# A two-layer decoder trunk in which stored weight remainders change queue and an out-projection's gates, next norm and first mixes change place

## The chip, the cores and the metric

The kernel runs on one core of a Trainium2 chip. The time is the device time of one execution in microseconds (us); the number to predict is the median of several executions. The program works with five engines, each with an instruction queue of its own that is worked through in order: TensorE (PE in the profile, its weight loads PEld), VectorE (DVE), ScalarE (ACT), GpSimd (POOL) and SyncE (SP, which only issues DMAs).

## What is computed

The input has 512 tokens of width 1024; 16 learned meta tokens are put ahead, which makes 528 rows. There are two layers, each with a half-weighted SwiGLU block, a mixer and another such block, with an RMS norm ahead of each. The mixer of layer 0 is RWKV-7 time mixing, that of layer 1 sparse attention. The change lies in layer 0:

```python
xx = shift(h) - h
xr, xw, xk, xv, xa, xg = h + xx * mix          # six mixes of the normed rows
r, k, v = xr @ w_r, xk @ w_k, xv @ w_v
w_log = -softplus(-(w0 + tanh(xw @ w1) @ w2)) - 0.5
a = sigmoid(a0 + (xa @ a1) @ a2)
g = sigmoid(xg @ g1) @ g2                      # the gate
y = wkv7_scan(...)
out = ((norm(y) + bonus) * g) @ w_o            # gate, then out-projection
```

All is float32 in and out.

## The kernel before

**Numbers as pairs.** A float32 product is made of three matmuls in a faster 32-bit format (`mm3`, line 597): each operand x is split into a rounded part hi (ScalarE copies x into the format) and the remainder lo (VectorE subtracts hi from x), and w_hi x_hi, w_hi x_lo and w_lo x_hi are added in one PSUM bank. The tokens are worked in two ranges, A (272 rows) and B (256 rows), channels down the partitions, so a matmul has a 128x128 weight block and 272 or 256 columns.

**Weights** (class `Weights`, from line 201). All weights lie in DRAM as units of 128x1024, in the order in which TensorE takes them, eight blocks to a unit. A unit is loaded by SP into one of four buffers `wraw`, ScalarE writes `whi`, VectorE writes `wlo` (four buffers each); `take` (line 271) splits two units ahead of use, three where a store is near. Some units are used again later in the program. For these, `wlo` is computed once and stored in DRAM (tiles `lo...`), and later loaded instead of being computed (`back`, line 256; groups `lo<-wlo` and `wlo<-lo` of the profile). There are 32 such stores: 12 of units that the first block uses itself (kind "keep"), 14 of projection units that are split early, between the first block's own units, and only stored there (kind "save", every fourth place of the order from unit 27), and 6 of out-projection units ("keep"). A `wlo` buffer that is stored is free for its next unit only when the store has landed. The store is issued in `split` (line 253) right behind the subtraction. 26 of the stores lie in the first 210 us, the other 6 in the first out-projection.

**Order.** The text of the program is the order of every engine. A planner (`run`, line 862, with the model `Clock`) puts the steps of side chains between the matmuls of a main stream. `early` (line 890) puts the statistics of the next norm into a stream: at step `at` the column sums (`Norm.stat`: matmuls with `ones` into a `bg` bank, then a Newton iteration of some 12 small VectorE instructions on a tile `nst`), and some steps later (`apart`) the spread to 128 partitions (matmuls with `ident`, copied by ScalarE into `rstd`).

**The out-projection** (`outproj`, line 1488) is called for range A in `joined` (line 1579), after the second half of a SwiGLU block for range B, and later for range B. `gate(m)` makes five matmuls into one of three `bg` banks, VectorE multiplies the bank with the scan's result (tile `AR`) into a tile `tb`, and `split` writes hi (ScalarE, rows `p<-tb` of ACT) and lo (VectorE, rows `p<-tb,p` of DVE). Gates 0, 1 and 2 come first; then for d = 0 to 7 gate d+3 and the nine matmuls of block d into three `acc` banks (columns m = 0, 1, 2); then columns 3 to 7, each with 24 matmuls into one `acc` bank. There are four `acc` banks, used in turn. At the end of a column VectorE adds the bank to the residual stream (rows `h<-acc,h`, called h0 to h7 here), ScalarE squares it and VectorE adds the square to `ss`.

**The next projection** (`proj`, line 948) starts inside that stream: `joined` takes a step of it at three places of the out-projection. Each of these steps makes one mix (`mix`, line 964): VectorE norms a channel block (`ynat<-h,vecs,rstd`), subtracts (`bu<-ynat`) and mixes (`tb<-bu,vecs,ynat`); hi and lo follow in the next two mixes. When the out-projection is done, the projection takes its four accumulators from the four `acc` banks, which columns 4, 5, 6 and 7 of the out-projection used last, and for each channel block d it does 12 matmuls, three for each accumulator.

Of the kernel before, what the change touches and what calls it, by code (L numbers as in the profile page):

```python
# [10 lines left out]
F32 = mybir.dt.float32  # L11
F32R = mybir.dt.float32r
I32 = mybir.dt.int32
AF = mybir.ActivationFunctionType
# [11 lines left out]
B = (272, 528)  # L26
# [25 lines left out]
def blk(key, k, m):  # L52
    return (key, k, m * 128, (m + 1) * 128)
# [149 lines left out]
class Weights:  # L203
# [35 lines left out]
    def split(self, last):  # L239

        while self.nlo <= min(last, len(self.units) - 1):
            u = self.nlo
            self.round(u)
            self.back(u)
            r = self.raw.pop(u)
            w = r.shape[1]
            if self.kind[u] != "again":
                lo = self.pool.tile([128, 1024], F32R, name="wlo", bufs=self.bufs)
                self.nc.vector.tensor_sub(lo[:, :w], r, self.hi[u][:, :w].bitcast(F32))
                self.lo[u] = lo  # L250
            if self.kind[u] in ("save", "keep"):
                d = self.saved[self.key[u]] = self.dram.tile([128, 1024], F32, name=f"lo{self.key[u]}")
                self.nc.sync.dma_start(d, lo.bitcast(F32))
            self.nlo += 1

    def back(self, last):
# [278 lines left out]
def trunk(ctx, tc, wall, plan, h0, vec, cstd, gqk, out, stop=None, gap=0.0, share=400.0, slack=200.0, fulls={}):  # L535
    clock = Clock()
    nc = Core(tc.nc, clock)
    @contextmanager
    def tile_pool(name, bufs=1, **kw):
        with tc.tile_pool(name=name, bufs=bufs, **(kw if "space" in kw else dict(reuse_waits="tile", **kw))) as pool:  # L540
            yield Pool(pool, bufs, clock)
# [46 lines left out]
    def col(c):  # L588
        return vecs[:, c:c + 1]

    def bank():
        return psum.tile([128, 512], F32, name="acc", bufs=4)

    def bbank(tag="bg"):
        return psum.tile([128, 512], F32, name=tag, bufs={"bg": 3, "ry": 1}[tag])

    def mm3(p, w, x, first, last):

        nc.tensor.matmul(p, w[0], x[0], start=first, stop=False)
        nc.tensor.matmul(p, w[0], x[1], start=False, stop=False)  # L600
        nc.tensor.matmul(p, w[1], x[0], start=False, stop=last)

    def split(hi, lo, src):
        nc.scalar.activation(hi, src, AF.Copy)
        nc.vector.tensor_sub(lo, src, hi.bitcast(F32))
# [103 lines left out]
    def residual(m, r, p, c):  # L709
        s = slice(*r)  # L710
        nc.vector.scalar_tensor_tensor(h[:, m, s], p, c, h[:, m, s], op0=OP.mult, op1=OP.add)
# [178 lines left out]
    def early(main, norm, r, at=12, X=None, start=0, every=4, apart=0):  # L890


        steps = spread = None
        due = 10 ** 6
        own = Chain(None)

        def mine(f, *a):
            clock.chain = own
            x = f(*a)
            clock.chain = None  # L900
            return x

        for i, c in enumerate(main):
            if i == at:
                spread = mine(norm.stat, r)
            elif i > at + apart and spread and own.ready + gap < clock.t["tensor"]:
                spread = mine(spread)
                due = i + 3
            if X and i >= start and i > at and not spread and (own.ready - 800 <= clock.t["tensor"] or i >= due):
                steps = steps or norm.steps(X(), r)  # L910
                mine(next, steps, None)
                due = i + every
            yield c
        if spread:
            spread()
        if X:
            steps = steps or norm.steps(X(), r)
            for _ in steps:
                pass


    class Range:
# [14 lines left out]
        def spread(self, dst, p, f, **kw):  # L937

            nc.scalar.activation(dst[:, :8], chunks(p[:, :256]), f, **kw)
            if self.pad:  # L940
                nc.scalar.activation(dst[:, 8, :self.pad], p[:, 256:], f, **kw)
# [3 lines left out]
    def chunks(ap):  # L945
        return ap.rearrange("p (c t) -> p c t", t=CH)

    def proj(R, norm, pairs, core, ahead, park=None):

        r, pad, nch = R.r, R.pad, R.nch  # L950
        n = R.n - pad
# [10 lines left out]
        xm, slot, late = {}, {}, []  # L962
# [29 lines left out]
        def mixes(k):  # L992
            while k and queue and pairs.free:
                i, d = queue.pop(0)
                if i == 2:
                    norm.apply(d, r, hn[d][:, 1:1 + n])
                    nc.vector.tensor_sub(xx[d // 4][:, d % 4, :n], hn[d][:, 0:n], hn[d][:, 1:1 + n])
                mix(i, d)
                if (i, d) == (5, 3) and park:
                    park.move(nc, core.tile([128, 2, 2, 256], F32R, name="bu", bufs=2))  # L1000
                if not queue:
                    R.have.add("mixed")
                if i == 2 and pad and d % 4 == 3:
                    nc.scalar.activation(hnlast[:, d - 3:d + 1], hn2[d // 4][:, :, n:n + 1], AF.Copy)
                k -= 1
# [19 lines left out]
        if pad:  # L1025
            for t in (R.BKV[:, :, 8, 1:3, pad:], R.P[:, :, 8, 1 + pad:], R.a[:, :, n:288]):
                nc.gpsimd.memset(t, 0.0)
        for _ in range(4 if park else 3):
            mixes(1)
            yield  # L1030

# [43 lines left out]
        for kind, *st in proj_steps():  # L1075
# [19 lines left out]
            elif kind == "lora":  # L1095
                key, d = st
# [15 lines left out]
            else:  # L1112
                d = st[0]
# [374 lines left out]
    def outproj(R, pairs, nxt, last=None):  # L1488

        r = R.r  # L1490
        n = R.n - R.pad
        shi, slo = (t for _, t in R.gates)
        xs, slot = {}, {}

        def gate(m):
            p = bbank()
            mm3(p[:, :n], W.take(blk("g2", 0, m)), (shi[:, 0, :n], slo[:, 0, :n]), True, False)
            w = W.take(blk("g2", 1, m))
            nc.tensor.matmul(p[:, :n], w[0], shi[:, 1, :n], start=False, stop=False)
            nc.tensor.matmul(p[:, :n], w[1], slo[:, 1, :n], start=False, stop=True)  # L1500
            t = work.tile([128, 288], F32, name="tb", bufs=4)
            y = R.AR[:, m, :, 1]
            nc.vector.scalar_tensor_tensor(chunks(t[:, :256]), y[:, :8], col(LNB + m), chunks(p[:, :256]),
                                           op0=OP.add, op1=OP.mult)
            if R.pad:
                nc.vector.scalar_tensor_tensor(t[:, 256:n], y[:, 8, :R.pad], col(LNB + m), p[:, 256:n],
                                               op0=OP.add, op1=OP.mult)
            slot[m] = pairs.take()
            xs[m] = [slot[m][1][:, j, :n] for j in range(2)]
            split(*xs[m], t[:, :n])  # L1510

        def end(m, p):
            residual(m, r, p[:, :n], 1.0)
            nxt.add(m, r)

        for m in range(3):
            gate(m)
            yield
        ps = [bank() for _ in range(3)]
        for d in range(DT):  # L1520
            if d + 3 < DT:
                gate(d + 3)
            if d + 3 == DT - 1:
                for t in R.gates:
                    pairs.give(t)
                if last:
                    last()
            for m in range(3):
                mm3(ps[m][:, :n], W.take(blk("wo", d, m)), xs[d], d == 0, d == DT - 1)
            yield  # L1530
        for m in range(3):
            end(m, ps[m])
        for m in range(3, DT):
            p = bank()
            for d in range(DT):
                mm3(p[:, :n], W.take(blk("wo", d, m)), xs[d], d == 0, d == DT - 1)
                if m == DT - 1:
                    pairs.give(slot[d])
                yield
            end(m, p)  # L1540


    norms = [Norm(i, "ry" if i == 2 else "bg") for i in range(6)]
# [35 lines left out]
    def joined():  # L1579

        main = proj(RB, norms[1], pairs, core, stepsA)
        for i, c in enumerate(early(outproj(RA, pairs, norms[2]), norms[1], B, at=9, apart=4)):
            if i in (27, 31, 35):
                assert B in norms[1].rstd
                next(main)
            yield c
        yield from early(main, norms[2], A, at=100, apart=16)

    mid, right = ExitStack(), ExitStack()
    pairs = Pairs(right.enter_context(tile_pool("pairs", side="right")), 14)  # L1590
# [5 lines left out]
    RA, RB = Range(A), Range(B)  # L1596
# [8 lines left out]
    def prefix(main):  # L1605
# [10 lines left out]
        for i, c in enumerate(main):  # L1616
# [7 lines left out]
            yield c  # L1624

    run(prefix(proj(RA, norms[1], pairs, core, stepsB, HB)), "pA")
    ffn_stage(0, 0, B, norms[1], "f00b", XB, stepsB, xdone=gates(RA), HID=HB, part="rest")
    drain()
# [12 lines left out]
    def first_x(main):  # L1641
# [8 lines left out]
        for _ in steps:  # L1650
            pass

    run(early(first_x(outproj(RB, pairs, norms[2], after)), norms[3], A, at=9, apart=4))
    right.close()
    xq = xa[0]

    hid = ctx.enter_context(tile_pool("hid"))
    at = ctx.enter_context(tile_pool("at"))
# [456 lines left out]
```

## Time and profile before

| | us |
|---|---|
| median of 3 runs | 2252.68 (2248.6 to 2252.9) |
| profiled execution | 2253.37 |
| its span | 2251.6 |
| TensorE busy | 2209.3 |
| VectorE busy | 1643.9 |
| ScalarE busy | 1261.6 |
| GpSimd busy | 70.5 |

The profile is one execution. A row of a timeline has the start in us, the length, engine, line, operation, tiles written and read, and how often it stands there in a row; in brackets the idle time of the engine before it, and what ended it. Every instruction of this program has line 387, a wrapper, so tiles tell them apart. Matmuls overlap, so from one start to the next is the time that one takes (0.126 us for 272 columns). DMA issues are on the queue of SP or POOL; "to landing" is from issue until the data is there.

### The profile page before, as it was taken

How to read it: one execution, taken by the hardware profiler on the slowest of the kernel's cores; microseconds unless marked ns; L12 is line 12 of the kernel's file. 1: busy time of each engine (PE TensorE's matmuls, PEld its weight loads, DVE VectorE, ACT ScalarE, POOL GpSimd, SP SyncE). 2: the span in 40 equal slices, each digit the busy share in tenths (PEclk: the TensorE clock that was granted, in tenths of full speed). 3: DMA queues.
4: the chain of work that ended last, by engine and by line, in shares of the span. 5: the costliest groups of instructions: out<-in, count | busy, mean ns of one | idle time of the engine just before them, and what ended most of it. 6: DMA issues, size and time to landing. Idle time of an engine off the chain costs nothing.

```text
span 2251.6 us, 49304 instructions
## 1 busy us (share of the span) xinstructions
PE 2209.3 (98%) x20028; PEld 2147.2 (95%) x20028; DVE 1643.9 (73%) x3281; ACT 1261.6 (56%) x2189; POOL 70.5 (3%) x122
## 2 busy tenths in 40 slices
PE   8999999999999999999999999999999999999999
PEld 8999999999899999999999999899998989989999
DVE  7777787846878883676656659887667988867665
ACT  6555784486478447654445445556545645555443
POOL 0000002011000110000000000000000000000000
PEclk9999999999999999999999999999999999999999
DMA  8788766622585562365555655553455543435654
GB/s 283 276 295 280 277 217 236 197 68 88 198 296 177 161 195 79 103 221 185 178 172 167 194 164 169 164 172 129 144 180 162 172 151 106 149 104 179 191 184 140
DMA packets 115188, 405.66 MB, mean 180 GB/s; under 512 B 12993, under 2 KB 17169, under 8 KB 114961
## 3 DMA queue, kind: packets, MB, share of 16 engines
q1 hardware_dynamic: 112592, 397.07, 53.0%
q0 software_dynamic: 2368, 5.44, 0.9%
q8 instruction: 157, 2.57, 0.5%
q14 instruction: 71, 0.57, 0.1%
HBM read 380.88 MB, written 21.05 MB: 179 GB/s over the span
## 4 chain that ended last, share of the span: by engine, by line
PE 82%; DVE 10%; ACT 4%; issue 2%; DMA 1%; SPq 0%; ACTq 0%; DVEq 0%
PE acc L387 70%; PE bg L387 9%; PE ry L387 4%; DVE wlo L387 3%; DMA wraw<-wall 1%; ACT whi L387 1%; DVE tb L387 1%; DVE ynat L387 1%; DVE p L387 1%; DVE rel L387 1%; DVE h L387 1%; DVE m L387 0%; ACT pr L387 0%; DVE AR L387 0%; ACT p L387 0%
## 5 line engine op out<-in xcount | busy, mean ns | idle before, releaser
L387 ACT ACTIVATE whi<-wraw 128x1024 fp32r<-128x1024 f32 (+2 forms) x674 | 705.6, 1052 | 412.0 <-PE acc L387 244.3
L387 DVE TENSOR_TENSOR wlo<-wraw,whi 128x1024 fp32r<-128x1024 f32 (+3 forms) x628 | 766.1, 1223 | 187.8 <-ACT whi L387 173.4
L387 PE MATMUL acc<-p,whi 128*128 128x272 f32 (+1 forms) x4112 | 790.0, 291 | 14.6 <-ACT whi L387 6.7
L387 PEld LDWEIGHTS acc<-p,whi 128*128 128x128 f32 x4112 | 644.9, 190 | 23.7 <-DVE p L387 7.2
L387 PE MATMUL acc<-p,wlo 128*128 128x272 f32 (+1 forms) x2056 | 590.4, 287 | 0.2 <-DVE wlo L387 0.2
L387 PEld LDWEIGHTS acc<-p,wlo 128*128 128x128 f32 x2056 | 389.8, 190 | 0.6 <-DVE wlo L387 0.6
L387 PE MATMUL acc<-xa_hi,whi 128*128 128x256 f32 (+1 forms) x1072 | 306.6, 286 | 0.0
L387 PE MATMUL acc<-xa_hi,wlo 128*128 128x256 f32 (+1 forms) x1072 | 304.3, 284 | 1.0 <-DVE wlo L387 1.0
L387 PE MATMUL acc<-xa_lo,whi 128*128 128x256 f32 (+1 forms) x1072 | 303.7, 283 | 0.0
L387 PE MATMUL acc<-hid_hi,whi 128*128 128x256 f32 (+1 forms) x880 | 253.0, 288 | 1.3 <-DVE ta L387 1.0
L387 PE MATMUL acc<-hid_lo,whi 128*128 128x256 f32 (+1 forms) x880 | 250.1, 284 | 4.3 <-DVE hid_lo L387 4.3
L387 PE MATMUL acc<-hid_hi,wlo 128*128 128x256 f32 (+1 forms) x880 | 249.9, 284 | 0.0
L387 PE MATMUL acc<-xb_hi,whi 128*128 128x256 f32 x744 | 211.3, 284 | 0.0
L387 PE MATMUL acc<-xb_hi,wlo 128*128 128x256 f32 x744 | 208.7, 280 | 0.0
L387 PE MATMUL acc<-xb_lo,whi 128*128 128x256 f32 x744 | 208.6, 280 | 0.0
L387 PEld LDWEIGHTS acc<-xa_hi,whi 128*128 128x128 f32 x1072 | 202.8, 189 | 1.6 <-issue 1.5
L387 PEld LDWEIGHTS acc<-xa_hi,wlo 128*128 128x128 f32 x1072 | 202.7, 189 | 1.4 <-DVE wlo L387 1.4
L387 PEld LDWEIGHTS acc<-xa_lo,whi 128*128 128x128 f32 x1072 | 203.0, 189 | 0.0
L387 PEld LDWEIGHTS acc<-hid_lo,whi 128*128 128x128 f32 x880 | 168.1, 191 | 5.2 <-DVE hid_lo L387 5.2
L387 PEld LDWEIGHTS acc<-hid_hi,whi 128*128 128x128 f32 x880 | 166.9, 190 | 3.9 <-issue 1.9
L387 DVE SCALAR_TENSOR_TENSOR h<-acc,h 128x256 f32<-128x256 f32 (+1 forms) x288 | 117.3, 425 | 71.5 <-PE acc L387 71.2
L387 PEld LDWEIGHTS acc<-hid_hi,wlo 128*128 128x128 f32 x880 | 167.2, 190 | 0.0
(309 smaller groups left out, 3156.9 us busy)
## 6 DMA issues: line engine op xcount, KB each, us to landing
wraw<-wall SPq DMA_DIRECT2D x659, 512.0 KB, 3.5
wlo<-lo SPq DMA_DIRECT2D x46, 512.0 KB, 4.4
lo<-wlo SPq DMA_DIRECT2D x32, 512.0 KB, 4.2
wraw<-wall SPq DMA_DIRECT2D x10, 438.0 KB, 3.3
out<-h SPq DMA_DIRECT2D x8, 256.0 KB, 2.3
h<-h SPq DMA_DIRECT2D x2, 512.0 KB, 8.1
L<-gm POOLq DMA_DIRECT2D x16, 64.0 KB, 2.4
ynat<-L POOLq DMA_DIRECT2D x2, 512.0 KB, 4.9
```

The costliest lines, as they stand in the source:

```text
L387: r = f(*args, **kw)
```

## The change

Four things are changed.

1. The 32 stores of lo parts are issued by GpSimd instead of SyncE.
2. In `outproj` the lo of a gate is no longer issued behind its hi, but behind the next gate's multiplication. The queue of VectorE so has gate m+1's product between the two.
3. In `joined`, the sums of the norm of range B are taken at step 5 instead of 9, four steps of the stream sooner, and with them the spread.
4. In `joined`, five steps of the projection (five mixes) are taken at steps 19, 24, 29, 34 and 39, in place of three at 27, 31 and 35; `proj` makes five single mixes for that.

```diff
             if self.kind[u] in ("save", "keep"):
                 d = self.saved[self.key[u]] = self.dram.tile([128, 1024], F32, name=f"lo{self.key[u]}")
-                self.nc.sync.dma_start(d, lo.bitcast(F32))
+                self.nc.gpsimd.dma_start(d, lo.bitcast(F32))
...
-        for _ in range(4 if park else 3):
+        for _ in range(4 if park else 5):
             mixes(1)
             yield
...
-        xs, slot = {}, {}
+        xs, slot, late = {}, {}, []
...
             slot[m] = pairs.take()
-            xs[m] = [slot[m][1][:, j, :n] for j in range(2)]
-            split(*xs[m], t[:, :n])
+            hi, lo = xs[m] = [slot[m][1][:, j, :n] for j in range(2)]
+            lower()
+            nc.scalar.activation(hi, t[:, :n], AF.Copy)
+            late.append(lambda: nc.vector.tensor_sub(lo, t[:, :n], hi.bitcast(F32)))
+
+        def lower():
+            while late:
+                late.pop()()
...
             if d + 3 < DT:
                 gate(d + 3)
+            else:
+                lower()
...
-        for i, c in enumerate(early(outproj(RA, pairs, norms[2]), norms[1], B, at=9, apart=4)):
-            if i in (27, 31, 35):
+        for i, c in enumerate(early(outproj(RA, pairs, norms[2]), norms[1], B, at=5, apart=4)):
+            if i in (19, 24, 29, 34, 39):
```

TensorE's order changes only in the place of the norm's small matmuls. The other engines change at three places.

The queue of VectorE at the start of the first out-projection; `tb<-AR,vecs,bg` is a gate's multiplication (256 and 16 columns), `p_...<-tb` its lo, numbers behind `p_` are buffers:

```order
 L387 SCALAR_TENSOR_TENSOR tb<-AR,vecs,bg 128x256
 L387 SCALAR_TENSOR_TENSOR tb<-AR,vecs,bg 128x16
+L387 SCALAR_TENSOR_TENSOR tb<-AR,vecs,bg 128x256
+L387 SCALAR_TENSOR_TENSOR tb<-AR,vecs,bg 128x16
 L387 TENSOR_TENSOR p_8021<-tb,p_8021 128x272
 L387 SCALAR_TENSOR_TENSOR tb<-AR,vecs,bg 128x256
 L387 SCALAR_TENSOR_TENSOR tb<-AR,vecs,bg 128x16
-L387 TENSOR_TENSOR p_8033<-tb,p_8033 128x272
+L387 TENSOR_TENSOR p_8032<-tb,p_8032 128x272
```

The multiplication of gate 0 keeps its place; that of gate 1 has moved ahead of gate 0's lo, and so on down the gates.

The queue of VectorE at the end of the first out-projection, before, from h5 to h7 (the three rows with `h`; `ynat`, `bu` and `tb` are a mix, `p_8352` is the lo of the first mix):

```order
L387 SCALAR_TENSOR_TENSOR h<-acc,h 128x272
L387 TENSOR_TENSOR ss<-ss,tb 128x272
L387 SCALAR_TENSOR_TENSOR ynat<-h,vecs,rstd 128x256
L387 TENSOR_TENSOR bu<-ynat 128x256
L387 SCALAR_TENSOR_TENSOR tb<-bu,vecs,ynat 128x256
L387 TENSOR_TENSOR p_8352<-tb,p_8352 128x256
L387 SCALAR_TENSOR_TENSOR h<-acc,h 128x272
L387 TENSOR_TENSOR ss<-ss,tb 128x272
L387 SCALAR_TENSOR_TENSOR h<-acc,h 128x272
```

The same place now, from the end of the fourth mix to h7 (`p_8337` and `p_8369` are the lo of the second and third mix; that of the first, `p_8313`, stands four rows higher):

```order
L387 SCALAR_TENSOR_TENSOR tb<-bu,vecs,ynat 128x256
L387 TENSOR_TENSOR p_8337<-tb,p_8337 128x256
L387 SCALAR_TENSOR_TENSOR h<-acc,h 128x272
L387 TENSOR_TENSOR ss<-ss,tb 128x272
L387 SCALAR_TENSOR_TENSOR ynat<-h,vecs,rstd 128x256
L387 TENSOR_TENSOR bu<-ynat 128x256
L387 SCALAR_TENSOR_TENSOR tb<-bu,vecs,ynat 128x256
L387 TENSOR_TENSOR p_8369<-tb,p_8369 128x256
L387 SCALAR_TENSOR_TENSOR h<-acc,h 128x272
L387 TENSOR_TENSOR ss<-ss,tb 128x272
L387 SCALAR_TENSOR_TENSOR h<-acc,h 128x272
```

Ahead of h5 there stood two mixes and no lo, and now there are four mixes and two lo; ahead of h6 and h7 three mixes and one lo, now five and three.

The queue of GpSimd in the first out-projection, where six of the stores now stand (`lo_...` is the DRAM tile, `gm` and `rs` are tiles of the next projection):

```order
 L387 MEMSET p_7906 64x272
 L387 MEMSET p_7907 128x272
+L387 DMA lo_8105<-wlo 128x1024
+L387 DMA lo_8167<-wlo 128x1024
+L387 DMA lo_8206<-wlo 128x1024
+L387 DMA lo_8255<-wlo 128x1024
+L387 DMA lo_8292<-wlo 128x1024
 L387 MEMSET gm 128x64
+L387 DMA lo_8352<-wlo 128x1024
 L387 MEMSET rs 128x288
```

Two memsets that stood free now wait behind stores, each of which waits for VectorE; the other 26 stores stand in the same way ahead of the memsets of the first projection.

## The prediction

> **What bounds the kernel now.** I read the page first, then the busy time in windows, then the timelines of TensorE and VectorE around the first out-projection, and last the waits and DMA rows of the first block.
>
> ```profile
> span 2251.6 us, 49304 instructions
> PE 2209.3 (98%) x20028; PEld 2147.2 (95%) x20028; DVE 1643.9 (73%) x3281; ACT 1261.6 (56%) x2189; POOL 70.5 (3%) x122
> ```
>
> TensorE is busy for all but 42.3 us of the span, and the change leaves it the same matmuls. So a gain can come only from idle time of TensorE or from a lowered clock. The profiled execution took 2253.37 us, 0.7 above the median of the runs; I sum against it and take the 0.7 off at the end. The windows show where idle time lies that this change can reach. A row has the window, its length, for five engines busy us and instructions, the granted clock, the DMA share and GB/s.
>
> ```profile
> 20.00:345.00 325.00, 321.78 (x2579) 319.10 (x2579) 256.19 (x466) 207.94 (x375) 6.43 (x7) 1.00 0.77 267
> 585.00:605.00 20.00, 18.00 (x126) 17.23 (x125) 15.21 (x38) 8.85 (x15) 0.00 (x0) 0.91 0.50 172
> 588.40:592.20 3.80, 3.80 (x19) 3.72 (x19) 2.64 (x9) 1.94 (x4) 0.00 (x0) 0.55 0.34 122
> 619.00:630.00 11.00, 8.33 (x43) 7.62 (x42) 9.88 (x25) 6.99 (x13) 0.00 (x0) 0.69 1.02 404
> 623.10:629.50 6.40, 5.89 (x26) 5.60 (x27) 6.12 (x16) 3.88 (x8) 0.00 (x0) 0.50 1.02 406
> 980.00:1003.00 23.00, 22.38 (x187) 22.01 (x186) 16.13 (x44) 11.90 (x22) 0.00 (x0) 1.00 0.70 255
> ```
>
> In the first 345 us, where 26 of the 32 stores lie, TensorE is idle for 3.2 us in all. At the start of the first out-projection (place 1) it is idle for 2.0 us and then runs 3.8 us at a clock of 0.55, which loses another 3.8 x 0.45 = 1.7. At its end (place 2) it is idle for 2.7 us, and 5.9 busy us at a clock of 0.50 lose 2.9. The second out-projection has 0.6 us. What waits for what at the two places, TensorE first:
>
> ```profile
> 587.77 0.49 PE L387 MATMUL bg<-p,whi 128*128 128x272 f32 x2 [1.82 <-DVE tb L387]
> ...
> 602.57 0.29 PE L387 MATMUL acc<-p,wlo 128*128 128x272 f32 x1
> ...
> 621.42 0.39 PE L387 MATMUL acc<-p,whi 128*128 128x256 f32 x1 [1.76 <-DVE p L387]
> ...
> 623.12 0.79 PE L387 MATMUL acc<-p,whi 128*128 128x256 f32 x2 [0.42 <-DVE h L387]
> ...
> 624.83 0.58 PE L387 MATMUL acc<-p,whi 128*128 128x256 f32 x1 [0.49 <-DVE p L387]
> ```
>
> ```profile
> 587.00 0.62 DVE L387 SCALAR_TENSOR_TENSOR tb<-AR,vecs,bg 128x256 f32<-128x256 f32 x2
> 588.12 0.44 DVE L387 TENSOR_TENSOR p<-tb,p 128x272 fp32r<-128x272 f32 x1 [0.50 <-ACT p L387]
> ...
> 601.83 0.44 DVE L387 TENSOR_TENSOR p<-tb,p 128x272 fp32r<-128x272 f32 x1 [0.50 <-ACT p L387]
> ...
> 606.16 0.78 DVE L387 SCALAR_TENSOR_TENSOR h<-acc,h 128x272 f32<-128x272 f32 x2
> ...
> 618.22 0.43 DVE L387 SCALAR_TENSOR_TENSOR h<-acc,h 128x272 f32<-128x272 f32 x1
> ...
> 621.29 0.43 DVE L387 SCALAR_TENSOR_TENSOR h<-acc,h 128x272 f32<-128x272 f32 x1
> ...
> 622.63 0.43 DVE L387 SCALAR_TENSOR_TENSOR h<-acc,h 128x272 f32<-128x272 f32 x1
> 622.98 0.48 DVE L387 SCALAR_TENSOR_TENSOR ynat<-h,vecs,rstd 128x256 f32<-128x256 f32 x1
> ...
> 624.36 0.42 DVE L387 TENSOR_TENSOR p<-tb,p 128x256 fp32r<-128x256 f32 x1
> ```
>
> At both places it is VectorE that is late. At place 1 gate 3 needs the first `bg` bank, which gate 0's multiplication frees (row 587.00). At place 2 the projection's first matmul waits for the lo of the first mix (row 621.42), the fourth accumulator for the bank that h7 frees (row 623.12, 0.49 us after the start of h7 at 622.63), and the second channel block for the next lo (row 624.83). VectorE is that late because it has not caught up since the gates: h0 starts at 606.16, though TensorE's last matmul into that bank started at 602.57 and took 0.29.
>
> **Gates pipelined.** Gate 0's multiplication keeps its place in VectorE's queue, so the wait of 1.82 us at gate 3 stays, and the low clock behind it. What goes is the 0.50 us for which VectorE stood before each of the eight lo (rows 588.12 to 601.83): 4.0 us of its time. TensorE was not waiting there, so this pays only through what VectorE does later.
>
> **Norm sums sooner.** The Newton steps move ahead of gate 6's product, and VectorE now meets them early. In the second out-projection, where its queue is less full, it stands for the sums like this:
>
> ```profile
> 998.13 0.16 DVE L387 TENSOR_SCALAR nst<-bg 91x3 f32<-91x3 f32 x1 [0.90 <-PE bg L387]
> ```
>
> That is 0.9 us given back, with gates 6 and 7 queued behind it. Also, a VectorE that is ahead will stand for gate 4's product, which TensorE makes at the low clock; no row shows this wait, and I take 0.5 us (one of the gates' waits), between 0 and 1.3. So h0 and all behind it come 4.0 - 0.9 - 0.5 = 2.6 us sooner; I keep 1.8 and 3.1 as ends. TensorE allows it: h0 could start at 602.9, which is 3.3 sooner.
>
> **Five mixes begun.** A mix is 1.38 us of VectorE from its first instruction to its lo (622.98 to 624.36), and the lo is 0.42. Ahead of h5, h6 and h7 alike there are now two more mixes and two more lo: 2 x 1.38 + 2 x 0.42 = 3.6 us. So
>
> - h5 moves from 618.22 to 618.22 - 2.6 + 3.6 = 619.2,
> - h6 from 621.29 to 622.3,
> - h7 from 622.63 to 623.6.
>
> The first lo is now made before h5, so the wait of 1.76 us goes. But the projection's second, third and fourth accumulators are the banks that h5, h6 and h7 free, each 0.49 after its start. TensorE ends the out-projection at about 619.4 (the first of the three waits is 1.76 before 621.42, and one matmul of the projection stands between), does the first accumulator, may go on with the second at 619.7, waits for the third until 622.8 and for the fourth until 624.1. Three matmuls at half clock, 0.6 us, and the second channel block starts at 624.7, against 624.83 before. A wait for lo has become a wait for banks of nearly the same end: 0.1 us gained, with the ends of VectorE's gain (3.1 and 1.8) from 0.6 sooner to 0.7 later. TensorE's idle time even grows, from 2.7 to some 3.6 us, so nothing speaks for a higher clock: the 2.9 us of low clock stay. Later VectorE is ahead, but nobody waited for it there.
>
> **Second out-projection.** It has the same pipelining; its 0.6 us is again gate 3's wait for gate 0. I count -0.1 us for small waits for lo.
>
> **Stores by GpSimd.** The rows of the first block and of DMA issues, one of POOL with the same size and direction:
>
> ```profile
> lo<-wlo SPq DMA_DIRECT2D x32, 512.0 KB, 4.2
> ...
> T<-ynat POOLq DMA_DIRECT2D x2, 512.0 KB, 4.1
> ```
>
> ```profile
> 207.65 0.33 SPq L387 DMA_DIRECT2D lo<-wlo  x1
> ```
>
> ```profile
> DVE wlo L387 <- DMA lo<-wlo: 11.6, 6, 2.6
> ```
>
> ```profile
> 185.44 1.23 DVE L387 TENSOR_TENSOR wlo<-wraw,whi 128x1024 fp32r<-128x1024 f32 x1 [2.35 <-DMA lo<-wlo]
> ```
>
> ```profile
> 188.73 0.29 PE L387 MATMUL acc<-p,wlo 128*128 128x272 f32 x1
> ```
>
> ```profile
> 221.65 0.44 DVE L387 TENSOR_TENSOR bu<-ynat 128x272 f32<-128x272 f32 x1
> ```
>
> SP loses 0.33 us of issue per store. The load behind a store waits for the same subtraction as the store, since that frees its `wraw` buffer, so loads come at most this bit sooner, and TensorE has only 3.2 us of idle time there. On the other side a store that lands later holds its `wlo` buffer: VectorE stood for that 6 times, 11.6 us in all. The worst kind is row 185.44, and the unit subtracted there was done at 186.67 and first used at 188.73: a cover of 2.1 us. I take 0, by the row of POOL (4.1 against 4.2); the ends are -1 us and the price of the slower rival. The memsets behind the 26 stores on POOL get 14 us: the last of these stores is issued at 207.65, the first tile so cleared is read at 221.65. Those of the first out-projection are for still later steps of the projection. I count nothing for either. The Trainium skill's page "DMA: Bandwidth & Descriptors" (section "SWDGE vs HWDGE vs iDMA") speaks against this edit: GpSimd's descriptors are written by software, and set-up is slower than on SP; its table puts the first byte at about 1 us instead of 0.6. No run here shows first bytes. By that, estimated, each store lands 0.4 us later, and the sum is the same, since the cover is larger.
>
> **Sum.** 0 (stores) + 0 (place 1) - 0.1 (place 2) - 0.1 (second out-projection) = -0.2 us against 2253.4, that is 2253.2 for the profiled execution and 2252.5 for the median. The runs before spread over 4.3 us, so about 0.2%, 4.5 us, is what a measurement of this kernel can tell from no change.
>
> **The rivals.** *Clock stays up at place 2.* The low clock came after 1.82 and 1.76 us of idle time, but whether a stretch is slowed may hang on when it falls. If it is not, the 2.9 us go: 2249.6, still within 0.2%. The Trainium skill's "TensorE: Matmul & The Clock Gate" (section "What's actually happening") says that the clock falls after an idle window of about 3.4 us, and that the window runs freely. By its length neither place would be slowed; the trace, with 0.55 after 1.82 us, disagrees. The free-running window fits this rival. Chance 0.16.
>
> *The banks do not hold* (faster). If VectorE gains all of 4.0 us and h5 to h7 do not come behind the new mixes in effect, place 2 loses neither 2.7 nor 2.9: 2252.5 - 5.6 = 2246.9. The order of VectorE's queue speaks against it, as the h rows stand behind the mixes. Chance 0.12.
>
> *Stores land late* (slower). The row of POOL is from a stretch with less traffic than the first block (DMA share 0.77 there). Each of the 14 stores that only keep a buffer busy lands one unit before that buffer is wanted; it costs TensorE what goes beyond the cover of 2.1 us, so it decides from a landing of 4.2 + 2.1 = 6.3 us. At 7.2 us it is 14 x 0.9 = 13 us: 2265. For it: VectorE already waits for stores there. Against: 4.1 us for POOL's own row. Chance 0.10.
>
> *The edits do not reach the waits they stand beside*: that is already the forecast for gate 3.
>
> **How the numbers follow.** Forecast 0.62, clock 0.16, banks 0.12, late stores 0.10. Predicted is the forecast's 2252.5. The range is 2246.5 to 2257: it takes in the banks rival and the clock rival, the spread of the runs and small losses of stores, and leaves out the rest of the slower one. Faster by over 0.2%: 0.12; within: 0.78; slower: 0.10.
>
> **What would show it.** Right: the wait of 1.8 us at gate 3 is still there; the eight waits of 0.50 us of VectorE are gone, and one for the sums has come; the projection's first matmuls wait, put down to `h` and not to `p`, 2 to 4 us in all; idle time in the first 345 us stays near 3.2 us, and stores land in 4 to 5 us. Wrong: TensorE goes from the out-projection into the projection without a wait of over 1 us, or the first block shows new waits for `wlo`.

## The result and the profile after

The changed kernel takes 2270.84 us (median of 5 runs, 2267.55 to 2273.94) against 2252.6 (5 runs); the ratio is 1.0089, 95% interval 1.0078 to 1.0101. So it is slower by 0.9%, some 18 to 20 us, where 2252.5 was forecast: outside the range, on the side of the late stores, and dearer than that rival's 2265. The profiled execution took 2267.55 us. Its page, the rows that answer to those of before:

```profile
span 2265.8 us, 49341 instructions
...
PE 2211.5 (98%) x20028; PEld 2148.4 (95%) x20028; DVE 1643.2 (73%) x3281; ACT 1260.2 (56%) x2189; POOL 86.6 (4%) x154
...
wlo<-lo SPq DMA_DIRECT2D x46, 512.0 KB, 4.9
lo<-wlo POOLq DMA_DIRECT2D x32, 512.0 KB, 6.2
```

TensorE's idle time has grown from 42.3 to 54.3 us, and a store lands 6.2 us after its issue where it took 4.2 on SyncE. The windows tell where (columns as before):

```profile
20.00:345.00 325.00, 310.62 (x2425) 306.50 (x2425) 238.31 (x442) 194.57 (x350) 16.40 (x36) 0.98 0.75 252
605.50:610.00 4.50, 4.24 (x33) 4.19 (x34) 4.50 (x14) 3.52 (x6) 0.00 (x0) 1.00 0.31 117
640.50:648.50 8.00, 7.94 (x54) 7.94 (x55) 7.79 (x22) 5.73 (x13) 0.00 (x0) 0.79 0.95 357
980.00:1003.00 23.00, 22.38 (x178) 22.04 (x178) 19.61 (x40) 12.96 (x23) 3.18 (x7) 1.00 0.55 175
```

In the first row TensorE stands for 14.4 us instead of 3.2, and its clock is 0.98 instead of 1.00. 154 matmuls that it did there before are not yet done. (The last row holds other work now, since everything stands later.) What TensorE, then VectorE, waited for in the first 345 us: total, times, longest.

```profile
PE acc L387 <- DVE wlo L387: 5.5, 4, 2.0
PE acc L387 <- DVE ta L387: 3.5, 1, 3.5
PE bg L387 <- DVE ss L387: 2.2, 1, 2.2
```

```profile
DVE wlo L387 <- issue: 19.1, 7, 4.3
DVE wlo L387 <- DMA lo<-wlo: 18.1, 5, 5.2
```

VectorE stood 5 times for a landing before it could write a `wlo`, 18.1 us (before: 6 times, 11.6). The seven waits put down to "issue" are new and of the same kind: each ends 0.08 us behind the landing of a store, as the rows at 145.28 and 156.44 below do. The three rows of TensorE are all waits for work that VectorE does behind these.

Two stretches of the timelines show the mechanism, VectorE's first and then GpSimd's. (`wlo<-wraw,whi` is the subtraction of a unit; the one that begins at 137.11 is a save unit.)

```profile
134.08 1.22 DVE L387 TENSOR_TENSOR wlo<-wraw,whi 128x1024 fp32r<-128x1024 f32 x1 [3.72 <-DMA lo<-wlo]
...
135.58 1.22 DVE L387 TENSOR_TENSOR wlo<-wraw,whi 128x1024 fp32r<-128x1024 f32 x1
137.11 1.23 DVE L387 TENSOR_TENSOR wlo<-wraw,whi 128x1024 fp32r<-128x1024 f32 x1 [0.31 <-ACT whi L387]
...
139.46 1.23 DVE L387 TENSOR_TENSOR wlo<-wraw,whi 128x1024 fp32r<-128x1024 f32 x1
...
145.28 1.23 DVE L387 TENSOR_TENSOR wlo<-wraw,whi 128x1024 fp32r<-128x1024 f32 x1 [4.24 <-issue]
...
156.44 2.36 DVE L387 TENSOR_TENSOR wlo<-wraw,whi 128x1024 fp32r<-128x1024 f32 x2 [1.67 <-issue]
```

```profile
88.54 0.53 POOL L387 DMA_DIRECT2D lo<-wlo  x1 [0.72 <-DVE wlo L387]
...
138.63 0.53 POOL L387 DMA_DIRECT2D lo<-wlo  x1 [10.49 <-DVE wlo L387]
150.18 0.53 POOL L387 DMA_DIRECT2D lo<-wlo  x1 [11.02 <-DVE wlo L387]
159.10 0.53 POOL L387 DMA_DIRECT2D lo<-wlo  x1 [8.39 <-DVE wlo L387]
...
222.21 0.53 POOL L387 DMA_DIRECT2D lo<-wlo  x1 [8.16 <-DVE wlo L387]
```

It is a loop. The save unit's store is issued at 138.63 and lands 6.57 us later (from the trace's record of that DMA), at 145.20; the second unit behind the save unit takes the same buffer and so begins at 145.28; the next save unit stands two subtractions behind that one, and its store waits for it. From the start of a unit that waited to the next store it is 138.63 - 134.08 = 4.55 us, so such a round takes the landing plus some 4.6 us. TensorE needs 9.16 for the three units of a round: before, 13 rounds lay between 88.61 (row below, of SyncE before) and 207.65. Now they lie between 88.54 and 222.21, which is 10.28 each. These 13 rounds cost 14.6 us.

Not all 13 are alike. In seven it is the second unit that begins right behind the landing, and these take 11.15 us each on average (4.1 to 4.9 us of it from that start to the next store). In four it is the third, as at 156.44 (two subtractions in a row, the second of them the save unit's): the next store follows after 159.10 - 156.44 = 2.7 us, and these rounds take 9.18, TensorE's own pace. The first and the last did not wait for a landing. So the seven cost 7 x 2.0 us, nearly all of the 14.6.

```profile
88.61 0.38 SPq L387 DMA_DIRECT2D lo<-wlo  x1
```

### The profile page after: what moved, and what is told of

It is laid out like the page before. It is cut to its first block, busy times and chain, and to the rows that moved or that the text cites. A ratio compares the mean times of both kernels' runs of the same rounds, so it can differ in the third digit from the quotient of the medians.

```text
span 2265.8 us, 49341 instructions
## 1 busy us (share of the span) xinstructions
PE 2211.5 (98%) x20028; PEld 2148.4 (95%) x20028; DVE 1643.2 (73%) x3281; ACT 1260.2 (56%) x2189; POOL 86.6 (4%) x154
## 4 chain that ended last, share of the span: by engine, by line
PE 76%; DVE 9%; issue 9%; ACT 4%; DMA 1%; POOL 1%; SPq 0%; DVEq 0%; ACTq 0%; POOLq 0%
PE acc L387 64%; PE bg L387 8%; PE ry L387 4%; DVE wlo L387 3%; ACT whi L387 1%; DVE tb L387 1%; DVE ynat L387 1%; DVE p L387 1%; DVE rel L387 1%; POOL lo L387 1%; DVE m L387 0%; DVE h L387 0%; DMA lo<-wlo 0%; ACT pr L387 0%; DMA h<-h 0%
```

## The experiments

Theory A is this loop. The medians below stand beside runs of the kernel before on the same chip: 2251.51 for the first four experiments, 2250.31 for the next four, 2250.47 for the last.

**Which part of the change costs.** `stores_only` is the kernel before with

```diff
-                self.nc.sync.dma_start(d, lo.bitcast(F32))
+                self.nc.gpsimd.dma_start(d, lo.bitcast(F32))
```

> The kernel before with one edit: the 32 stores are issued by GpSimd; the out-projection is that of before. Theory A (a loop: the store of a 'save' holds its wlo buffer, the second unit behind it waits for the landing, and the next save waits for that unit, so that a landing of 6.2 us instead of 4.7 and an issue 0.3 us later make the loop 10.3 us long where TensorE needs 9.2): the whole loss is here, 2268 to 2275 us, with saves issued 10.3 us apart. Rival B (the edits of the out-projections cost most of it): 2252 to 2256 us.

2271.39 us, ratio 1.009 (1.0072 to 1.0108): the whole loss, with the save units' stores 10.4 us apart. `stores_back` undoes the same line in the changed kernel.

> The changed kernel with one edit undone: the stores are issued by SyncE again. Theory A: the loss is gone and what the out-projection gave is left, 2249 to 2252.5 us; place 2 waits for banks (h) for 2 to 4 us. Rival B: 2265 us or more.

2249.93 us, ratio 0.9994 (0.9985 to 1.0003): the loss is gone, and the other three edits together make no difference that can be told. Rival B falls.

**Is it the buffer?** `own_buffers` keeps the stores on GpSimd and takes the save units out of the rotation of the four `wlo` buffers:

```diff
-                lo = self.pool.tile([128, 1024], F32R, name="wlo", bufs=self.bufs)
+                if self.kind[u] == "save":
+                    t = self.core.tile([128, 4, 1 + 288], F32, name="ynat", bufs=2)
+                    lo = t.rearrange("p a b -> p (a b)")[:, :1024].bitcast(F32R)
+                else:
+                    lo = self.pool.tile([128, 1024], F32R, name="wlo", bufs=self.bufs)
```

> The kernel before with the 32 stores issued by GpSimd, and the lo of the 14 save units written into two buffers of a tile that is unused until the projection, instead of the four wlo buffers. Landings stay at about 6 us, but no unit waits for the store of a save any more. Theory A: the loop is cut, 2249 to 2255 us, TensorE idle in 20 to 345 us under 5 us. Rival C (it is not the buffer: GpSimd's stores disturb the loads or VectorE whatever their buffer): 2264 us or more.

2249.21 us, ratio 0.999 (0.9981 to 0.9999). Its DMA rows, its window and what VectorE's subtractions wait for in the first 345 us (the one row of that kind; the helper's line is 391 here):

```profile
lo<-wlo POOLq DMA_DIRECT2D x18, 512.0 KB, 6.3
```

```profile
20.00:345.00 325.00, 322.53 (x2591) 320.37 (x2590) 257.60 (x467) 209.22 (x375) 20.65 (x38) 1.00 0.79 269
```

```profile
DVE wlo L391 <- ACT whi L391: 15.5, 22, 1.9
```

The stores land as late as in the changed kernel, and it costs nothing. (The 14 save stores stand in a row of their own there; from their issues and landings their mean is 6.54 us.) The 18 "keep" stores of this row, the six of the first out-projection among them, stay in the rotation on GpSimd, so theirs cost nothing either. Rival C falls. The save units' own buffers also leave the four `wlo` buffers to the other units, but this alone is no explanation: with the stores on SyncE, own buffers gain 1.7 us (`sums_own` against `sums_later`, below), not 22.

**Why does a store land late?** `scalar_queue` gives the stores to ScalarE (`nc.scalar.dma_start`), so that GpSimd has no part in them; the profile lists ScalarE's queue as hardware_dynamic, like SyncE's, and GpSimd's as software_dynamic.

> The kernel before with the 32 stores issued by ScalarE. Rival D (a store lands late on every queue but SP's, since it then competes with the loads): landing about 6 us and 2265 us or more. Theory A with the delay in GpSimd's own issue: landing 4 to 5 us as on SP, and 2251 to 2258 us, where the waits of ScalarE for the subtraction are the part above 2252.6.

2278.4 us, ratio 1.0116 (1.01 to 1.0132); rival D holds.

```profile
lo<-wlo ACTq DMA_DIRECT2D x32, 512.0 KB, 6.1
```

```profile
DVE wlo L387 <- DMA lo<-wlo: 30.5, 11, 4.6
```

The landing is as late as on GpSimd, so it is not GpSimd that is slow. (The time is 7 us above that on GpSimd. Of these, 4.6 are lost ahead of the first save unit, whose store is issued at 93.07 us instead of 88.44; the 13 rounds take 10.4 us each in both. The reason was not followed up.) Two runs then asked whether it is the place behind the loads. `load_first` leaves the stores on SyncE and issues the load that the same subtraction releases ahead of the store:

```diff
+                self.nlo += 1
+                while self.nraw < min(self.nlo + self.raw_bufs, len(self.units)):
+                    self.load()
+                self.nlo -= 1
                 self.nc.sync.dma_start(d, lo.bitcast(F32))
```

> The kernel before, stores still on SyncE, with two lines exchanged: the load that the same subtraction releases is issued ahead of the store instead of behind it. Theory E (a store lands early on SyncE only because it stands ahead of the next load in the same queue; on any other queue the two compete): landing 5.5 to 6.5 us, save units about 10 us apart, 2258 to 2272 us. Rival F (queues other than SyncE's are slow in themselves): landing at most 5 us, 2250 to 2256 us.

`loads_too` puts the first block's loads on GpSimd as well, behind the stores:

```diff
-        self.nc.sync.dma_start(r[:, :n], ...
+        (self.nc.gpsimd if 5 < u < 85 else self.nc.sync).dma_start(r[:, :n], ...
```

> The kernel before, with the stores and the weight loads of the first block both issued by GpSimd, the store ahead of the next load as on SyncE. Only the landings and the save units' distance in the first block are to be read, since the loads themselves may be later. Theory E: stores of the first block land in 4 to 5 us though GpSimd issues them. Rival F: 6 us as before.

The rows of the stores, `load_first` and then `loads_too`:

```profile
lo<-wlo SPq DMA_DIRECT2D x32, 512.0 KB, 6.1
```

```profile
lo<-wlo POOLq DMA_DIRECT2D x32, 512.0 KB, 4.7
```

This settles it for theory E. On SyncE's own queue, but behind a load, a store lands in 6.1 us; on GpSimd's queue, but ahead of the loads, in 4.7 (4.47 is the mean of the 26 of the first block). Early is whatever stands ahead of the next load in the load's own queue. The Trainium skill's page "DMA: Bandwidth & Descriptors" (section "Queues, rings and completion order") says that each DMA engine takes its queues in turn, packet by packet, and one queue's descriptors in order. These four landings agree with that: from another queue a store shares the engines with the loads. What the prediction drew from that page, software descriptors, is not what decides: the hardware queue of ScalarE is as late. One thing these runs leave open. On GpSimd the next load is issued 0.27 us ahead of the store in each of the 14 rounds, and on ScalarE at the same moment; a store on a queue of its own that is issued ahead of the load was not tried.

The times: `loads_too` 2255.13 (1.0013 to 1.0034), `load_first` 2254.04 (1.0007 to 1.0026). The second missed what theory E expected, 2258 to 2272 with save units 10 us apart (they are 9.1), and that corrects the theory: a late landing is not enough. VectorE in `load_first`; the second of the two subtractions at 122.14, and at 130.90, is a save unit.

```profile
122.14 2.36 DVE L391 TENSOR_TENSOR wlo<-wraw,whi 128x1024 fp32r<-128x1024 f32 x2 [2.70 <-DMA lo<-wlo]
...
125.63 1.23 DVE L391 TENSOR_TENSOR wlo<-wraw,whi 128x1024 fp32r<-128x1024 f32 x1 [0.78 <-ACT whi L391]
...
127.47 1.22 DVE L391 TENSOR_TENSOR wlo<-wraw,whi 128x1024 fp32r<-128x1024 f32 x1
...
130.90 2.37 DVE L391 TENSOR_TENSOR wlo<-wraw,whi 128x1024 fp32r<-128x1024 f32 x2 [1.86 <-DMA lo<-wlo]
```

```profile
133.66 0.43 SPq L391 DMA_DIRECT2D lo<-wlo  x1
```

Here the store stands one allocation later in the program, so its buffer should come free later in the order; in the trace it goes to the third unit behind the save unit, once to the fourth, and never to the second. The unit that waits (130.90) has the save unit right behind it, and from its start to the store it is 133.66 - 130.90 = 2.8 us instead of 4.6. With a landing of 6.3 a round is 9.1: TensorE's own pace, and TensorE is busy for 321.69 of the 325 us, as before. What `load_first` loses lies elsewhere (a wait of 2.2 us for a loaded lo at place 2 is new); not all of it was found.

**The out-projection's edits one by one**, stores on SyncE. `gates_alone` is the kernel before with `outproj` of the change; `mixes_alone` has the five mixes and the sooner sums, with `outproj` of before.

> The kernel before with the pipelined gates as its only edit. By the prediction's working VectorE reaches h0 some 3 to 4 us sooner, and here no mixes are put ahead of h5 to h7, so that this reaches place 2: its 2.7 us of waits shrink to under 1 and some of the low clock with it, 2246 to 2249 us. Rival: VectorE's 0.5 us waits at the gates were hidden, and place 2 is as before: 2250 to 2251 us.

> The kernel before with the two edits of the stream that joins out-projection and projection (sums of the norm at step 5, five mixes at steps 19 to 39), gates and stores as before. By the prediction's working h5 to h7 come later by 3.6 us less what the sooner sums give, and nothing is gained ahead of them: place 2 waits for banks for some 4 to 6 us in place of 2.7, 2251 to 2254 us. Rival (five mixes done ahead are worth more than the banks cost): under 2250 us.

2246.58 us, ratio 0.9983 (0.9974 to 0.9992), and 2254.64 us, 1.0016 (1.0008 to 1.0025). The first lies in its range and the second 0.6 us above, and they cancel. Gate 0 and h7 of `gates_alone`, and of `mixes_alone` (before: 587.00 and 622.63):

```profile
585.56 1.15 DVE L387 SCALAR_TENSOR_TENSOR tb<-AR,vecs,bg 128x256 f32<-128x256 f32 x4
...
618.64 0.43 DVE L387 SCALAR_TENSOR_TENSOR h<-acc,h 128x272 f32<-128x272 f32 x1
```

```profile
587.28 0.62 DVE L387 SCALAR_TENSOR_TENSOR tb<-AR,vecs,bg 128x256 f32<-128x256 f32 x2
...
626.32 0.43 DVE L387 SCALAR_TENSOR_TENSOR h<-acc,h 128x272 f32<-128x272 f32 x1
```

From gate 0 to h7 it was 35.63 us; with the pipelined gates it is 33.08, 2.6 us less (3 to 4 were expected), and with the mixes 39.04, 3.4 us more. (Gate 0 itself starts up to 1.7 us apart in these executions, ahead of all edits.)

The waits are not those expected. In `gates_alone` TensorE still waits 2.2 us at place 2 (under 1 was expected), and the clock, 1.00 here where it was 0.69, takes part in the gain:

```profile
619.00:630.00 11.00, 9.81 (x71) 8.79 (x72) 10.65 (x28) 6.51 (x13) 0.00 (x0) 1.00 1.02 408
```

In `mixes_alone` TensorE waits 1.7 us for `h` and 1.9 us for a loaded lo (4 to 6 us for banks were expected).

**What holds place 2.** In `stores_back` VectorE stands 0.56 us for ScalarE's square behind each residual. `sums_later` is `stores_back` with each square added one column later, behind the next residual; `sums_alone` has this edit alone in the kernel before.

```diff
+        sums = []
+        class Held:
+            @staticmethod
+            def later(_, f):
+                f() if f.__name__ == "square" else sums.append(f)
         def end(m, p):
             residual(m, r, p[:, :n], 1.0)
-            nxt.add(m, r)
+            while sums:
+                sums.pop()()
+            nxt.add(m, r, Held)
```

> The changed kernel with the stores back on SyncE and one more edit: VectorE adds the square of a column of the first out-projection to the norm's sum behind the next column's residual, so that it no longer stands about 0.56 us for each of six squares of ScalarE. If VectorE's work up to h7 is what holds place 2 (the theory of the prediction), h7 comes 3 to 4 us sooner, the waits for h of 1.5 us at place 2 go, and what is left is the wait for the first loaded lo: 2246 to 2249.5 us. If something else holds it (the loaded lo alone): no change from 2249.9.

> The kernel before with the sums of the squares put one column later as its only edit. If VectorE's work up to h7 and the first lo is what holds place 2, its 3.8 us of waits for squares pay here too: 2246 to 2248.5 us. If the five mixes of the change are needed for the gain of the run with both: 2249.5 us or more.

2243.98 us, ratio 0.9968 (0.9956 to 0.9981), and 2247.4, 0.9984 (0.9975 to 0.9992). TensorE's waits from 580 to 640 us in `stores_back`, and in `sums_later`:

```profile
PE bg L387 <- DVE tb L387: 1.8, 1, 1.8
PE acc L387 <- DMA wlo<-lo: 1.8, 1, 1.8
PE acc L387 <- DVE h L387: 1.5, 2, 0.9
PE acc L387 <- DVE p L387: 0.5, 1, 0.5
```

```profile
PE bg L387 <- DVE tb L387: 1.8, 1, 1.8
PE acc L387 <- DMA wlo<-lo: 0.9, 1, 0.9
PE acc L387 <- DVE p L387: 0.5, 1, 0.5
```

The waits for `h` are gone, and from gate 0 to h7 it is 33.0 us instead of 36.5: VectorE's queue up to h7 held place 2. The waits alone make 2.4 us; the clock from 615 to 632 us is also higher, 1.00 instead of 0.80, and by how much the shorter waits are the cause of that is not shown. Last, `sums_own` adds the own buffers to `sums_later`, and `sums_own_pool` is that with the stores on GpSimd.

> The same with the save units' lo in two buffers of their own, stores on SyncE: the best version so far if both hold. The sum of the two: 2244 to 2248 us. If the own buffers gain nothing where the store lands early (the loop of before was not late): as the run beside it.

> The best version so far (changed kernel, sums later, own buffers for the save units) with the stores on GpSimd again. Theory A with order in the queue: the stores land at about 6 us, nothing waits for them, 2241.5 to 2245 us as with SyncE. If the stores still cost where nobody waits for their buffer: 2250 us or more.

2242.24 us, ratio 0.9967 (0.9954 to 0.998), and 2242.08, 0.9962 (0.9949 to 0.9974). These are the best versions; with own buffers the queue of the stores makes no difference. Whether the five mixes still pay in them was not tried.

## Why the prediction was wrong

- **Stores, taken at 0: the step that failed.** It failed twice. First the landing: I took POOL's row of 4.1 us, and in the first block it is 6.2. The prediction's own word against that row, less traffic, is not what sets it apart. The first of its two transfers, before, has this window:

```profile
431.90:436.10 4.20, 4.20 (x38) 4.20 (x37) 2.99 (x4) 1.43 (x3) 0.56 (x1) 1.00 0.91 301
```

  The DMA share is 0.91 while it is under way (0.69 over the 20 us around it, and 0.77 over the first block). What differs more is the neighbours. That transfer is issued with one load under way, 1.4 us behind its issue and 1.0 us ahead of the next. The stores of the save units on GpSimd are issued 0.27 us behind a load, with 2.4 transfers under way on average.

  Second the cover, which also made the rival's price too low. "It costs TensorE what goes beyond the cover of 2.1 us" counts that cover afresh for each of the 14 stores, and puts the deciding landing at 6.3 us; by that sum the landings of now (the 14 have a mean of 6.42, and are issued 0.3 us later than on SyncE) would cost 14 x 0.4 = 6 us. But a unit that comes late delays the next save unit, and so the next store: the cover is a stock that is spent once. What counts is the round, landing plus 4.4 us on SyncE (4.55 and 0.08 from landing to start, less the 0.26 us by which GpSimd issues later), against TensorE's 9.16. For a round in which the second unit waits, the deciding landing is then about 4.8 us. The 14 of before have a mean of 4.65: they were at that edge, which the 11.6 us of VectorE's waits could have told.
- **Size.** A round of 6.42 + 4.6 = 11.0 us would cost 13 x 1.9 = 24 us if the second unit waited in each. Measured are 14.6, since that is so in seven only. Further on it is 18.2: TensorE's wait of 0.8 us that ended at 356.93 us ends at 375.16. The wait for `ss` (2.2 us, 0.2 before) and a clock of 0.50 over the 3.4 us from 234.20 on, which loses 1.7, make up the difference. Counted on TensorE over the whole block, it is 11.2 us more of idle time and 0.02 x 325 = 6.5 us of clock.
- **Place 1: right.** Gate 3's wait is still there, 1.8 us in `stores_back`.
- **VectorE's gain in the gates: right.** 4.0 - 0.9 - 0.5 was forecast. In `stores_back` h0 comes 16.22 us after gate 0 (586.58 and 602.80), where it was 19.16: 2.9 us sooner, and 2.6 was forecast. None of the eight waits of 0.50 is left, and these two have come:

```profile
591.44 0.62 DVE L387 SCALAR_TENSOR_TENSOR tb<-AR,vecs,bg 128x256 f32<-128x256 f32 x2 [0.37 <-PE bg L387]
...
595.33 0.16 DVE L387 TENSOR_SCALAR nst<-bg 128x2 f32<-128x2 f32 x1 [0.89 <-PE bg L387]
```

- **Place 2: right in its mechanism.** In `stores_back`, VectorE's h5 to h7 and TensorE's first matmuls of the projection:

```profile
618.67 0.43 DVE L387 SCALAR_TENSOR_TENSOR h<-acc,h 128x272 f32<-128x272 f32 x1
...
621.74 0.43 DVE L387 SCALAR_TENSOR_TENSOR h<-acc,h 128x272 f32<-128x272 f32 x1
...
623.09 0.43 DVE L387 SCALAR_TENSOR_TENSOR h<-acc,h 128x272 f32<-128x272 f32 x1
```

```profile
620.54 0.39 PE L387 MATMUL acc<-p,wlo 128*128 128x256 f32 x1 [1.81 <-DMA wlo<-lo]
...
622.23 0.60 PE L387 MATMUL acc<-p,whi 128*128 128x256 f32 x2 [0.94 <-DVE h L387]
...
623.58 0.79 PE L387 MATMUL acc<-p,whi 128*128 128x256 f32 x2 [0.54 <-DVE h L387]
```

Forecast were 619.2, 622.3 and 623.6 for h5 to h7, and waits for the third and fourth bank until 622.8 and 624.1; all stand 0.5 us sooner, most of it because the whole stretch does. The two waits for banks make 1.5 us (3.5 with the stores on GpSimd), where 2 to 4 were named. What I had not seen is the first wait, for a loaded lo: with the other wait gone it is late next. The second out-projection has its 0.6 us of wait as before. The edits together measure 0.9985 to 1.0003; -0.2 us was forecast.
- **The rivals.** Late stores (0.10) was the one, with the right place and too small a price. The banks held. The clock: in the profiled execution after, place 1 ran at 1.00 (0.55 before) and place 2 still at 0.79 over 8 us, so a stretch is not slowed in every execution. (It is clearest in `sums_alone`, where gate 3's wait is 1.81 us as before and place 1 runs at 1.00.) In the profiled execution the two places give back 2.8 of the 18.2 us.

## What to carry to other kernels

A buffer that waits for its store, while the next store waits for the buffer's next user, makes a loop: add up one round and hold it against the pace of the engine to be fed; slack per use says nothing. Moving a transfer to another engine's queue does not only save issue time: it gives up its place ahead of the loads, here 2 us of landing, so look at which transfers stand next to it in the queue and at who waits for the landing. Where the loop can't be made shorter, give the stored tile a buffer of its own, or let its next user be one unit later.

## What the hardware showed

- The order in one queue mattered more than the kind of queue: 4.2 us on SyncE ahead of the load, 6.1 behind it, 6.2 on GpSimd, 6.1 on ScalarE, 4.7 on GpSimd with the loads behind.
- GpSimd issues a store 0.29 us after the subtraction's end (mean of the 26), SyncE 0.03.
- Wherever the granted clock falls in one of the 14 traces, it falls to 0.50, for 3.41 or 6.83 us (a stretch at the very end of each aside). At place 1 it did so behind five of the six waits of 1.81 to 1.84 us, and behind none of the six of 1.58 to 1.60.
- Executions of one kernel go with their mean granted clock: of the 19 runs of before beside the first four experiments, the eight at 0.997 or more took 2248.9 to 2250.4 us, the eleven at 0.996 or less 2251.3 to 2254.4. Beside the later experiments the two groups overlap, with means of 2249.6 against 2251.5 and 2251.6.
